# Gate tiles of a hybrid decoder layer in seven block products, and branch block sums spread over their turns

## Chip, cores and metric

The kernel runs on one core of one Trainium2 chip. The metric is the device time of one execution in microseconds; the kernel before takes 2350.80 us (median of 3 runs, 2350.69 to 2352.27). All data is fp32. Matrix products are made of three matmuls each (high x high, high x low, low x high), after an operand has been split into a rounded high part and the rest.

## What is computed

One decoder layer over 16 meta tokens and 1024 tokens, model width 1024. Cut to what matters here:

```python
h = rms_norm(x, norm1_w)
(rq, rk, rv, rg, dq, dk, dv, cb, cc, cx, gates) = [h @ w_in[:, s:e] for s, e in column_bounds()]
ret  = retention(...) ; diff = diff_attention(...) ; conv = cb * short_conv(cc * cx, conv_w)
g = sigmoid(gates).reshape(b, l, 3, 1024)
merged = g[:, :, 0] * (ret @ w_branch[0]) + g[:, :, 1] * (diff @ w_branch[1]) + g[:, :, 2] * (conv @ w_branch[2])
x = x + merged @ w_out
u = square(relu(rms_norm(x, norm2_w) @ w_up))
y = rms_norm(x + u @ w_down, final_norm_w)
```

The gates are 3 x 1024 columns of the input projection: 24 gate tiles of 128 channels by 1024 tokens.

## The kernel before

Everything is kept transposed: channels on the 128 partitions, tokens along the row. There are two ways to make a matrix product.

**Direct.** `gemm` (with `kstep`, L163 to L165) makes 128 channels by 512 tokens in 8 k-steps of 3 matmuls, so 24 matmuls; a gate tile is two of these, 48 matmuls. The weights come through `weights`: two DMAs of 256 KB each on SP's queue, a cast on ScalarE (L135), a subtraction on VectorE (L136). The right-hand side is `H`, the input times norm weight, split. The per-token factor `R` is applied to the result by `scaled` (L252).

**Seven block products.** Class `Quad` makes four tiles (4 x 128 channels by 1024 tokens) as two pairs `p`. A pair's product is a 2 x 2 block product, made with seven products of combined blocks instead of eight. The right-hand side is needed as seven combined blocks in `ORDER = ("B11", "B21", "T1", "B22", "T2", "T3", "T4")`, each split, in two 1024 KB tiles (`op`). One product of both pairs is a *turn*: 24 matmuls (L843 to L845). A quad is seven turns, 168 matmuls. `prep` combines and splits the weights two turns ahead, `copy` and `evac` take sums out of PSUM (L849 on ScalarE, L863 on VectorE), `use` does what follows.

From the gates on, the program has two parts.

The **gate stage** (24 direct tiles, in the order that the tile framework's scheduler finds) also makes the combined blocks of the three branch results for the branch products: `branch_sums(br, k)`, twelve calls, one behind each second gate tile. A call loads four 256 KB blocks, makes T1 to T4 with four VectorE operations, splits five of the seven blocks, and stores 3 MB through POOL's queue to `TD`. Gates go to `GD`. In the stage's second half the first four operands of the first branch product (`SET`) are loaded on SP's queue.

From L1243 on, the **order is written out by hand**. `steps` holds the turns; the loop at the end issues, for each turn `s`: what takes the last turn's results, the turn's matmuls, the weight preparation of turn `s + 2`, then `work[s]`, the loads of turn `s + 3`, then `fetch[s]`. Each engine runs its instructions in that order and waits at the first that isn't ready. `turn_over` loads the next right-hand side on POOL's queue while the last quad of the one before runs; T3 and T4 come whole and are split by `work` entries. The first steps are the six branch quads (branch 2, 1, 0), then the output projection, the MLP and the last product.

Rings of buffers tie the queues together: `raw` 10, `w` 5, `X` 16, `g` 3, `k` 2. A buffer that a DMA stores from is free when the store has landed.

Of the kernel before, what the change touches and what calls it, by code (L numbers as in the profile page):

```python
# [16 lines left out]
ALU = mybir.AluOpType  # L17
# [54 lines left out]
def trunk_kernel(ctx: ExitStack, tc, x, w_in, w_branch, w_out, w_up, w_down, w_down2, w_down3, vecs, lam_in, consts, y):  # L72
# [33 lines left out]
    def f32(ap):  # L106
        return ap.bitcast(F32)
# [614 lines left out]
    def ready(br, k, n, src):  # L722
        w = temp("w", [P, 2, 512], F32R)
        split(src, w[:, 0], w[:, 1])
        nc.gpsimd.dma_start(out=TD[br][n][:, :, k], in_=f32(w))

    def branch_sums(br, k):
        src = dict(BR)[br]
        b = {}
        for z in range(2):  # L730
            for j in range(2):
                b[z, j] = temp("raw", [P, 512])
                nc.sync.dma_start(out=b[z, j], in_=src[:, 4 * z + k, half(j)])
        for n, zj in PLAIN.items():
            ready(br, k, n, b[zj])
# [6 lines left out]
        for n, t in (("T3", t3), ("T4", t4)):  # L742
            nc.gpsimd.dma_start(out=TD[br][n][:, k], in_=t)
        ready(br, k, "T1", t1)
        ready(br, k, "T2", t2)

    turns[:] = TURNS
    last_sig = None
    SET = {}
    sums_todo = [(br, k) for br, _ in BR for k in range(4)]  # L750
    for n, (br, f) in enumerate((br, f) for br, _ in BR for f in range(KT)):
        wt = weights(w_in[G_GATE + br * KT + f], lo_eng=v)
        for c0, w in CH_TOK:
            pt = gemm(wt, H, c0, w)
            gt = slot("t2", [P, 512])
            scaled(gt, pt, c0, w)
            last_sig = a.activation(out=gt, in_=gt, func=AF.Sigmoid)
            nc.gpsimd.dma_start(out=GD[br][:, f, c0 - META:c0 - META + w], in_=gt)

        with tc.issue_after(getattr(last_load[0], "ins", last_load[0])):  # L760
            if n % 2 == 1:
                branch_sums(*sums_todo.pop(0))
            if 10 <= n < 18 and n % 2 == 0:

                name = ORDER[(n - 10) // 2]
                SET[name] = [opnd(True, [P, 4, 512]) for _ in range(2)]
                for z in range(2):
                    nc.sync.dma_start(out=f32(SET[name][z]), in_=TD[2][name][:, z])
# [19 lines left out]
    def at(table, s, fn):  # L788
        table.setdefault(s, []).append(fn)
# [171 lines left out]
    def last_load(name):  # L961
        open_op(SET, name, 4, False)
        if name in READY:
            for z in range(2):
                G.dma_start(out=f32(SET[name][z]), in_=TD[2][name][:, z])
        else:
            G.dma_start(out=f32(SET[name][1]), in_=TD[2][name])

    def last_split(name):
        oh, ol = SET[name]  # L970
        for k in range(4):
            split(f32(ol[:, k]), oh[:, k], ol[:, k])

    for i, name in enumerate(ORDER[4:]):
        at(fetch, i, lambda name=name: last_load(name))
        if name not in READY:
            at(work, 2 + i, lambda name=name: last_split(name))
# [143 lines left out]
    now = [0]  # L1121

    spare = [0]

    def pick_h():
        spare[0] += 1
        return "gggkk"[spare[0] % 5]
# [247 lines left out]
```

## Time and profile before

| | before |
|---|---|
| median of 3 runs | 2350.80 us |
| profiled execution | 2350.85 us |
| its span (first to last instruction) | 2348.8 us |
| TensorE busy (PE) | 2293.8 us, 98% |
| VectorE busy (DVE) | 1599.6 us, 68% |
| ScalarE busy (ACT) | 1071.3 us, 46% |
| GpSimd busy (POOL) | 496.9 us, 21% |
| DMA over the whole span | 337.57 MB, 144 GB/s |

The page's slices show PE at 9 tenths or more almost everywhere, so a time is read as a number of matmuls and what lies between them. The gate stage runs to 1346.6 us of the span, the first branch product starts at 1347.35 us. DMA is light until the gate stage and heaviest there.

### The profile page before, as it was taken

How to read it: one execution, taken by the hardware profiler on the slowest of the kernel's cores; microseconds unless marked ns; L12 is line 12 of the kernel's file. 1: busy time of each engine (PE TensorE's matmuls, PEld its weight loads, DVE VectorE, ACT ScalarE, POOL GpSimd, SP SyncE). 2: the span in 40 equal slices, each digit the busy share in tenths (PEclk: the TensorE clock that was granted, in tenths of full speed). 3: DMA queues.
4: the chain of work that ended last, by engine and by line, in shares of the span. 5: the costliest groups of instructions: out<-in, count | busy, mean ns of one | idle time of the engine just before them, and what ended most of it. 6: DMA issues, size and time to landing. Idle time of an engine off the chain costs nothing. (4 is left out here: it accounts for less than half of the span.)

```text
span 2348.8 us, 32974 instructions
## 1 busy us (share of the span) xinstructions
PE 2293.8 (98%) x11854; PEld 1992.6 (85%) x11854; DVE 1599.6 (68%) x3276; ACT 1071.3 (46%) x2079; POOL 496.9 (21%) x666
## 2 busy tenths in 40 slices
PE   7999999999999999999999999999989999999997
PEld 7999999999999899898888787778867778788876
DVE  7776777777766466667545467685776676876776
ACT  6644644654634333333333333343455565643434
POOL 2232132232221321212323210100002242200003
PEclk9999999999999999999999999999999999999999
DMA  3111111111111111114998866736425566865352
GB/s 140 33 54 38 50 54 37 55 44 44 53 42 46 54 45 46 64 55 162 336 375 329 290 247 231 309 107 206 157 66 177 186 228 246 326 232 207 108 197 72
DMA packets 126885, 337.57 MB, mean 144 GB/s; under 512 B 15744, under 2 KB 19968, under 8 KB 118144
## 3 DMA queue, kind: packets, MB, share of 16 engines
q1 hardware_dynamic: 84912, 159.27, 20.2%
q0 software_dynamic: 41808, 176.19, 19.7%
q8 instruction: 93, 1.52, 0.3%
q14 instruction: 72, 0.59, 0.1%
HBM read 224.24 MB, written 111.15 MB: 143 GB/s over the span
## 5 line engine op out<-in xcount | busy, mean ns | idle before, releaser
L163 PE MATMUL pmm<-H,whi 128*128 128x512 f32 (+3 forms) x1640 | 574.3, 352 | 12.4 <-ACT H L198 8.2
L164 PE MATMUL pmm<-H,whi 128*128 128x512 f32 (+3 forms) x1640 | 574.2, 351 | 1.4 <-DVE H L199 1.3
L165 PE MATMUL pmm<-H,wlo 128*128 128x512 f32 (+3 forms) x1640 | 573.5, 351 | 0.0
L843 PE MATMUL pb<-op,w 128*128 128x512 f32 x1176 | 465.7, 396 | 28.2 <-DVE t L863 24.2
L845 PE MATMUL pb<-op,w 128*128 128x512 f32 x1176 | 462.7, 393 | 0.0
L844 PE MATMUL pb<-op,w 128*128 128x512 f32 x1176 | 462.5, 393 | 0.0
L136 DVE TENSOR_TENSOR w<-raw,w 128x512 fp32r<-128x512 f32 (+1 forms) x400 | 263.3, 670 | 203.7 <-ACT w L135 200.9
L135 ACT CAST w<-raw 128x512 fp32r<-128x512 f32 (+1 forms) x400 | 237.4, 604 | 308.3 <-PE pb L845 111.3
L163 PEld LDWEIGHTS pmm<-H,whi 128*128 128x128 f32 x1640 | 309.5, 189 | 38.1 <-ACT H L198 8.2
L164 PEld LDWEIGHTS pmm<-H,whi 128*128 128x128 f32 x1640 | 310.4, 189 | 26.8 <-DVE H L199 2.1
L165 PEld LDWEIGHTS pmm<-H,wlo 128*128 128x128 f32 x1640 | 310.0, 189 | 24.2
L136 POOL TENSOR_TENSOR wlo<-raw,whi 128x512 fp32r<-128x512 f32 x142 | 194.0, 1367 | 593.1 <-ACT whi L135 548.1
L843 PEld LDWEIGHTS pb<-op,w 128*128 128x128 f32 x1176 | 221.8, 189 | 85.2 <-DVE t L863 20.3
L845 PEld LDWEIGHTS pb<-op,w 128*128 128x128 f32 x1176 | 221.8, 189 | 51.2 <-DVE w L136 0.9
L844 PEld LDWEIGHTS pb<-op,w 128*128 128x128 f32 x1176 | 222.0, 189 | 49.4 <-issue 0.2
L135 ACT CAST whi<-raw 128x512 fp32r<-128x512 f32 x192 | 118.7, 619 | 185.6 <-issue 69.8
L849 ACT COPY t<-pb 128x512 f32<-128x512 f32 x132 | 75.9, 584 | 109.4 <-PE pb L845 109.1
L820 DVE TENSOR_TENSOR raw<-raw,raw 128x512 f32<-128x512 f32 (+1 forms) x176 | 111.7, 664 | 10.3 <-DMA raw<-w_branch 8.6
L1133 POOL DMA_DIRECT2D d<-X x124 | 66.3, 540 | 231.4 <-DVE X L1169 119.2
L863 DVE TENSOR_TENSOR t<-pb,t 128x512 f32<-128x512 f32 x132 | 90.0, 686 | 16.3 <-PE pb L845 9.6
L380 ACT ACTIVATE B<-B,nb 128x144 f32<-128x144 f32 (+3 forms) x64 | 50.6, 791 | 99.4 <-DVE nb L379 99.2
L896 POOL DMA_DIRECT2D op<-d x46 | 24.6, 539 | 280.4 <-PE pb L845 278.5
(295 smaller groups left out, 3764.5 us busy)
## 6 DMA issues: line engine op xcount, KB each, us to landing
op<-d POOLq DMA_DIRECT2D x59, 1024.0 KB, 8.5
raw<-w_in SPq DMA_DIRECT2D x192, 256.0 KB, 2.6
d<-X POOLq DMA_DIRECT2D x140, 256.0 KB, 4.0
d<-w POOLq DMA_DIRECT2D x60, 512.0 KB, 6.7
raw<-w_up SPq DMA_DIRECT2D x76, 256.0 KB, 3.4
raw<-w_down SPq DMA_DIRECT2D x56, 256.0 KB, 5.4
d<-t POOLq DMA_DIRECT2D x50, 256.0 KB, 5.7
raw<-d SPq DMA_DIRECT2D x48, 256.0 KB, 7.5
```

Of the source, the lines that this page charges most:

```text
L135: a.copy(out=hi, in_=src)
L136: (eng or v).tensor_tensor(out=lo, in0=src, in1=f32(hi), op=ALU.subtract)
L163: nc.tensor.matmul(pt, lhsT=hi[:, s], rhs=xh[:, c0:c0 + w], start=start, stop=False)
L164: nc.tensor.matmul(pt, lhsT=hi[:, s], rhs=xl[:, c0:c0 + w], start=False, stop=False)
L165: nc.tensor.matmul(pt, lhsT=lo[:, s], rhs=xh[:, c0:c0 + w], start=False, stop=stop)
L820: comb = lambda d, x0, x1, o: v.tensor_tensor(out=d, in0=x0, in1=x1, op=o)
L843: nc.tensor.matmul(pt, lhsT=w[0][:, s], rhs=b[0][:, k], start=first, stop=False, skip_group_check=True)
L844: nc.tensor.matmul(pt, lhsT=w[0][:, s], rhs=b[1][:, k], start=False, stop=False, skip_group_check=True)
L845: nc.tensor.matmul(pt, lhsT=w[1][:, s], rhs=b[0][:, k], start=False, stop=k == nk - 1, skip_group_check=True)
L849: a.copy(out=t, in_=pt)
L863: v.tensor_tensor(out=sb, in0=pt, in1=sb, op=ALU.add)
L1133: at(fetch, now[0] + 1, lambda: G.dma_start(out=dst, in_=src))
```

## The change

Four gate tiles (the first four of branch 2) stay direct. Behind them the block sums of the *input* are made: `input_sums(k)` loads x again, multiplies by the norm weight and by `R`, makes T1 to T4, splits all seven blocks; the first four stay on the chip (`HS`), T2, T3, T4 go to DRAM (`HD`) and come back through POOL's queue. The other 20 gate tiles become five quads of the written-out order, ahead of the branch quads, with the sigmoid in `use`. The branch sums become twelve `branch_unit`s of nine operations each, dealt to the turns by the list `ROOM`; each part is stored by DMAs of 256 KB (12 a unit). The operands of the first branch product come by `turn_over` while the last gate quad runs.

```diff
-    for n, (br, f) in enumerate((br, f) for br, _ in BR for f in range(KT)):
-        wt = weights(w_in[G_GATE + br * KT + f], lo_eng=v)
+    for f in range(4):
+        wt = weights(w_in[G_GATE + 2 * KT + f], lo_eng=v)
...
         with tc.issue_after(getattr(last_load[0], "ins", last_load[0])):
-            if n % 2 == 1:
-                branch_sums(*sums_todo.pop(0))
-            if 10 <= n < 18 and n % 2 == 0:
...
+            for k in ((0, 1), (2,), (3,), ())[f]:
+                input_sums(k)
...
+    def input_sums(k):
+        b = {}
+        for z in range(2):
+            for j in range(2):
+                b[z, j] = temp("raw", [P, 512])
+                nc.sync.dma_start(out=b[z, j], in_=x[:, 4 * z + k, META + j * 512:META + j * 512 + 512])
+        for z in range(2):
+            for j in range(2):
+                f = 4 * z + k
+                v.scalar_tensor_tensor(out=b[z, j], in0=b[z, j], scalar=vec[:, V_N1 + f:V_N1 + f + 1],
+                                       in1=R[:, META + j * 512:META + j * 512 + 512], op0=ALU.mult, op1=ALU.mult)
...
+        for n, t in (("B11", b[0, 0]), ("B21", b[1, 0]), ("T1", t1), ("B22", b[1, 1])):
+            split(t, HS[n][0][:, k], HS[n][1][:, k])
...
+        for n, t in (("T2", t2), ("T3", t3), ("T4", t4)):
+            w = temp("w", [P, 2, 512], F32R)
+            split(t, w[:, 0], w[:, 1])
+            nc.gpsimd.dma_start(out=HD[n][:, :, k], in_=f32(w))
...
+    for i, name in enumerate(ORDER[4:]):
+        at(fetch, i, lambda name=name: input_load(name))
+    for br, quad in ((2, 1), (1, 0), (1, 1), (0, 0), (0, 1)):
+        q = Quad(pairs_of(w_in[G_GATE + br * KT:G_GATE + (br + 1) * KT], quad), 4, HS, gate_use(br, quad))
+        for i in range(7):
+            product_step(q, i)
...
+        def parts(n, src):
+            u = src()
+            h = temp(pick_h(), [P, 512])
+            split(u, h.bitcast(F32R), u.bitcast(F32R))
+            put(TD[br][n][:, 0, k], h)
+            put(TD[br][n][:, 1, k], u)
...
+    ROOM = (3, 1, 3, 3, 5, 2, 4)
...
+            at(fetch, turn - 2, load)
+            for fn in ops:
+                while room == 0:
+                    turn += 1
+                    room = ROOM[turn % 7]
+                at(work, turn, fn)
+                room -= 1
...
+    turn_over(len(steps) - 7, SETS[2], 4, lambda name: TD[2][name], READY, FIRST)
```

How the order moves, at the places that matter. First VectorE (DVE) behind the second direct gate tile's first half (the `scaled` of that half leads both pieces; `raw` are loaded blocks, `wlo` gate weights). Before:

```order
L252 TENSOR_TENSOR t22167_12153<-pmm2166_12128,R25_117 128x512
L136 TENSOR_TENSOR w2174_12194<-raw2170_12186,w2174_12194 128x512
L737 TENSOR_TENSOR raw2177_12206<-raw2171_12188,raw2170_12186 128x512
L136 TENSOR_TENSOR w2175_12198<-raw2172_12190,w2175_12198 128x512
L136 TENSOR_TENSOR wlo2181_12230<-raw2181_12227,whi2181_12229 128x512
L136 TENSOR_TENSOR w2176_12202<-raw2173_12192,w2176_12202 128x512
```

and of the change:

```order
L252 TENSOR_TENSOR t22194_12238<-pmm2193_12213,R25_117 128x512
L736 SCALAR_TENSOR_TENSOR raw2175_12127<-raw2175_12127,vec_79,R25_117 128x512
L736 SCALAR_TENSOR_TENSOR raw2176_12129<-raw2176_12129,vec_79,R25_117 128x512
L736 SCALAR_TENSOR_TENSOR raw2177_12131<-raw2177_12131,vec_79,R25_117 128x512
L136 TENSOR_TENSOR op2159_12047<-raw2175_12127,op2158_12046 128x512
L739 TENSOR_TENSOR raw2179_12139<-raw2176_12129,raw2175_12127 128x512
L136 TENSOR_TENSOR wlo2206_12317<-raw2206_12314,whi2206_12316 128x512
```

Where branch sums and gate work alternated, the input sums of all four k begin. Second, VectorE where the direct tiles end and the products begin (`w2465` before, `w2260` in the change, is the first weight block of the first product). Before:

```order
L740 TENSOR_TENSOR raw2420_14127<-raw2420_14127,raw2423_14133 128x512
L741 TENSOR_TENSOR raw2422_14131<-raw2422_14131,raw2420_14127 128x512
L252 TENSOR_TENSOR t22411_14024<-pmm2410_13999,R25_117 128x512
L136 TENSOR_TENSOR w2429_14158<-raw2420_14127,w2429_14158 128x512
L136 TENSOR_TENSOR w2465_14214<-raw2463_14210,w2465_14214 128x512
L136 TENSOR_TENSOR wlo2415_14066<-raw2415_14063,whi2415_14065 128x512
L252 TENSOR_TENSOR t22413_14053<-ps2412_14028,R25_117 128x512
```

and of the change:

```order
L136 TENSOR_TENSOR w2203_12300<-raw2200_12277,w2203_12300 128x512
L743 TENSOR_TENSOR raw2214_12384<-raw2214_12384,raw2212_12380 128x512
L136 TENSOR_TENSOR w2204_12304<-raw2199_12275,w2204_12304 128x512
L744 TENSOR_TENSOR raw2211_12378<-raw2211_12378,raw2214_12384 128x512
L745 TENSOR_TENSOR raw2213_12382<-raw2213_12382,raw2211_12378 128x512
L136 TENSOR_TENSOR w2216_12403<-raw2211_12378,w2216_12403 128x512
L136 TENSOR_TENSOR w2217_12407<-raw2214_12384,w2217_12407 128x512
L136 TENSOR_TENSOR w2218_12411<-raw2213_12382,w2218_12411 128x512
L136 TENSOR_TENSOR w2260_12536<-raw2258_12532,w2260_12536 128x512
```

Before, the first product's weights are split while direct tiles are still evacuated; in the change they stand behind the last input sum: 69 operations from the first L736 to `w2260`, both included, 61 of them to `w2203`. Third, POOL's queue where operands of a branch product are loaded (`op`, 1024 KB each, here T1 to T3); all other rows are stores of 256 KB. Before:

```order
L896 DMA op2563_14722<-d2146_12034 128x2048
L896 DMA op2564_14723<-d2146_12034 128x2048
L896 DMA op2572_14766<-d2147_12035 128x2048
L896 DMA op2573_14767<-d2147_12035 128x2048
L909 DMA op2594_14865<-d2149_12037 128x2048
```

and of the change (`op2613` is T3 of the first branch product, `d2154` holds blocks of the last branch):

```order
L891 DMA op2601_14389<-d2141_12029 128x2048
L962 DMA d2157_12045<-X2597_14379 128x512
L962 DMA d2152_12040<-k2598_14381 128x512
L891 DMA op2602_14390<-d2141_12029 128x2048
L904 DMA op2613_14447<-d2142_12030 128x2048
L928 DMA d2136_12024<-t2580_14303 128x512
L962 DMA d2155_12043<-g2605_14428 128x512
L962 DMA d2154_12042<-g2607_14433 128x512
```

Before, the loads follow each other alone; in the change they stand among the branch sums' stores and the gates' stores.

## Rows read from the trace of the kernel before

**Rows 1.** Page, part 1: busy time, share of the span, instructions of each engine

```profile
PE 2293.8 (98%) x11854; PEld 1992.6 (85%) x11854; DVE 1599.6 (68%) x3276; ACT 1071.3 (46%) x2079; POOL 496.9 (21%) x666
```

**Rows 2.** Timeline of PE: start us, duration us, engine, line, operation, [idle before <-releaser]

```profile
1096.77 0.39 PE L165 MATMUL pmm<-H,wlo 128*128 128x512 f32 x1
1097.46 0.39 PE L163 MATMUL ps<-H,whi 128*128 128x512 f32 x1
...
1101.62 0.39 PE L163 MATMUL ps<-H,whi 128*128 128x512 f32 x1
...
1346.17 0.40 PE L165 MATMUL pmm<-H,wlo 128*128 128x512 f32 x1
1347.35 0.50 PE L843 MATMUL pb<-op,w 128*128 128x512 f32 x1 [0.78 <-DVE t L252]
...
1350.25 0.39 PE L843 MATMUL pb<-op,w 128*128 128x512 f32 x1
...
1354.33 0.39 PE L843 MATMUL pb<-op,w 128*128 128x512 f32 x1
```

**Rows 3.** Windows: us; busy us (count) by engine; PEclk, DMA share, GB/s: gate stage, full-share stretches

```profile
1090.00:1347.00 257.00, 256.57 (x1110) 208.18 (x1109) 132.98 (x208) 91.73 (x155) 80.58 (x132) 1.00 0.92 334
1104.00:1128.00 24.00, 24.00 (x106) 19.50 (x105) 16.15 (x26) 10.22 (x18) 10.92 (x18) 1.00 1.02 391
1136.00:1160.00 24.00, 24.00 (x105) 19.50 (x105) 13.76 (x22) 9.16 (x16) 8.63 (x15) 1.00 1.00 349
1200.00:1232.00 32.00, 32.00 (x141) 25.99 (x140) 13.62 (x21) 9.79 (x17) 8.10 (x14) 1.00 1.02 399
1400.00:1432.00 32.00, 32.00 (x140) 26.07 (x139) 13.35 (x20) 7.48 (x13) 4.45 (x9) 1.00 1.02 411
```

**Rows 4.** Window of the first branch quads, columns as in Rows 3

```profile
1347.00:1546.00 199.00, 194.51 (x836) 156.27 (x837) 142.61 (x222) 70.71 (x125) 15.52 (x29) 1.00 0.66 246
```

**Rows 5.** Timeline of DVE, SP and ACT where the first branch sums begin

```profile
1097.20 0.69 DVE L252 TENSOR_TENSOR t<-pmm,R 128x512 f32<-128x512 f32 x1 [4.49 <-PE pmm L165]
1097.56 3.65 SPq L733 DMA_DIRECT2D raw<-d  x8
1100.37 0.62 ACT L135 CAST w<-raw 128x512 fp32r<-128x512 f32 x1 [7.59 <-DMA raw<-d]
1102.21 0.62 ACT L135 CAST w<-raw 128x512 fp32r<-128x512 f32 x1 [0.69 <-DMA raw<-d]
```

**Rows 6.** Timeline of DVE: operations back to back, merged (x2, x3)

```profile
1684.07 1.89 DVE L136 TENSOR_TENSOR w<-raw,w 128x512 fp32r<-128x512 f32 x3
1687.47 1.41 DVE L1073 SCALAR_TENSOR_TENSOR X<-X,vec,k 128x512 f32<-128x512 f32 x2
```

**Rows 7.** Groups by line and shape: count | busy us, mean ns | idle before

```profile
L1073 DVE SCALAR_TENSOR_TENSOR X<-X,vec,k 128x512 f32<-128x512 f32 x16 | 11.2, 747 | 0.0
```

**Rows 8.** DMA issues: out<-in, queue, count, KB each, median us from issue to landing

```profile
d<-w POOLq DMA_DIRECT2D x60, 512.0 KB, 6.7
d<-A POOLq DMA_DIRECT2D x8, 512.0 KB, 2.9
```

**Rows 9.** Page, part 5: ScalarE casts of a split, and POOL's issue of a 256 KB store

```profile
L135 ACT CAST w<-raw 128x512 fp32r<-128x512 f32 (+1 forms) x400 | 237.4, 604 | 308.3 <-PE pb L845 111.3
L1133 POOL DMA_DIRECT2D d<-X x124 | 66.3, 540 | 231.4 <-DVE X L1169 119.2
```

**Rows 10.** Timeline of PE: the longest idle time between products

```profile
1719.68 0.77 PE L843 MATMUL pb<-op,w 128*128 128x512 f32 x1 [8.04 <-DVE t L863]
```

**Rows 11.** Windows around that idle time, columns as in Rows 3

```profile
1716.00:1720.00 4.00, 0.32 (x1) 0.35 (x2) 4.00 (x7) 0.43 (x1) 0.00 (x0) 0.57 0.45 133
1720.00:1724.00 4.00, 4.00 (x12) 3.10 (x12) 0.82 (x2) 2.49 (x5) 0.00 (x0) 0.58 0.02 4
1724.00:1728.00 4.00, 4.00 (x19) 3.23 (x18) 2.44 (x5) 3.57 (x7) 0.00 (x0) 1.00 0.36 99
```

More of the change, by code (lines that the diff above doesn't have):

```diff
@@ L720, in trunk_kernel @@
     TD = {br: {n: dram([P, 2, 4, 512] if n in READY else [P, 4, 512]) for n in ORDER} for br, _ in BR}
[L722 to L728, printed above, removed]
+    FIRST = ORDER[:4]
+    HS = {n: [opnd(True, [P, 4, 512]) for _ in range(2)] for n in FIRST}
+    HD = {n: dram([P, 2, 4, 512]) for n in ORDER[4:]}
+    def input_sums(k):
         b = {}
@@ L732, in branch_sums @@
                 b[z, j] = temp("raw", [P, 512])
-                nc.sync.dma_start(out=b[z, j], in_=src[:, 4 * z + k, half(j)])
-        for n, zj in PLAIN.items():
-            ready(br, k, n, b[zj])
+                nc.sync.dma_start(out=b[z, j], in_=x[:, 4 * z + k, META + j * 512:META + j * 512 + 512])
[4 more added lines that the diff above has]
+                                       in1=R[:, META + j * 512:META + j * 512 + 512], op0=ALU.mult, op1=ALU.mult)
         t1 = temp("raw", [P, 512])
         v.tensor_tensor(out=t1, in0=b[0, 1], in1=b[0, 0], op=ALU.subtract)
+        for n, t in (("B11", b[0, 0]), ("B21", b[1, 0]), ("T1", t1), ("B22", b[1, 1])):
+            split(t, HS[n][0][:, k], HS[n][1][:, k])
         t3, t2, t4 = b[1, 1], b[0, 0], b[1, 0]
@@ L741, in branch_sums @@
         v.tensor_tensor(out=t4, in0=t4, in1=t2, op=ALU.subtract)
[L742 to L745, printed above, removed]
+        for n, t in (("T2", t2), ("T3", t3), ("T4", t4)):
+            w = temp("w", [P, 2, 512], F32R)
+            split(t, w[:, 0], w[:, 1])
+            nc.gpsimd.dma_start(out=HD[n][:, :, k], in_=f32(w))
     turns[:] = TURNS
-    last_sig = None
-    SET = {}
-    sums_todo = [(br, k) for br, _ in BR for k in range(4)]
-    for n, (br, f) in enumerate((br, f) for br, _ in BR for f in range(KT)):
-        wt = weights(w_in[G_GATE + br * KT + f], lo_eng=v)
+    for f in range(4):
+        wt = weights(w_in[G_GATE + 2 * KT + f], lo_eng=v)
         for c0, w in CH_TOK:
@@ L756, in trunk_kernel @@
             scaled(gt, pt, c0, w)
-            last_sig = a.activation(out=gt, in_=gt, func=AF.Sigmoid)
-            nc.gpsimd.dma_start(out=GD[br][:, f, c0 - META:c0 - META + w], in_=gt)
+            a.activation(out=gt, in_=gt, func=AF.Sigmoid)
+            nc.gpsimd.dma_start(out=GD[2][:, f, c0 - META:c0 - META + w], in_=gt)
         with tc.issue_after(getattr(last_load[0], "ins", last_load[0])):
-            if n % 2 == 1:
-                branch_sums(*sums_todo.pop(0))
-            if 10 <= n < 18 and n % 2 == 0:
[L765 to L768, printed above, removed]
+            for k in ((0, 1), (2,), (3,), ())[f]:
+                input_sums(k)
     gates.close()
@@ L925, in pairs_of, with gate_use, use, pick_h @@
         return [[w[2 * p + r][:, half(z)] for r in range(2) for z in range(2)] for p in (2 * quad, 2 * quad + 1)]
+    def gate_use(br, quad):
+        def use(p, r, j, src):
+            f = 4 * quad + 2 * p + r
+            g = temp("X", [P, 512]) if (r, j) == (1, 0) else src
+            a.activation(out=g, in_=src, func=AF.Sigmoid)
+            at(fetch, now[0] + 1, lambda: G.dma_start(out=GD[br][:, f, half(j)], in_=g))
+        return use
+    now = [0]
+    spare = [0]
+    def pick_h():
+        spare[0] += 1
+        return "gggkk"[spare[0] % 5]
@@ new lines, in input_load @@
+    def input_load(name):
+        open_op(HS, name, 4, False)
+        for z in range(2):
+            G.dma_start(out=f32(HS[name][z]), in_=HD[name][:, z])
+    for i, name in enumerate(ORDER[4:]):
[4 more added lines that the diff above has]
+            product_step(q, i)
+    at(work, len(steps) + 1, lambda: a.preload_act_table_set("natural_log_exp_and_others"))
@@ new lines, in branch_unit, with load, put, comb @@
+    def branch_unit(br, k):
+        b, t = {}, {}
+        def load():
+            for z in range(2):
+                for j in range(2):
+                    b[z, j] = temp("X", [P, 512])
+                    nc.sync.dma_start(out=b[z, j], in_=dict(BR)[br][:, 4 * z + k, half(j)])
+        def put(dst, src):
+            at(fetch, now[0], lambda: G.dma_start(out=dst, in_=src))
+        def parts(n, src):
[4 more added lines that the diff above has]
+            put(TD[br][n][:, 1, k], u)
+        def comb(n, x0, x1, op, out=None):
+            x0, x1 = x0(), x1()
+            t[n] = out() if out else temp("X", [P, 512])
+            v.tensor_tensor(out=t[n], in0=x0, in1=x1, op=op)
+            if n in ("T3", "T4"):
+                put(TD[br][n][:, k], t[n])
+        B = lambda z, j: lambda: b[z, j]
+        W = lambda n: lambda: t[n]
+        return load, [lambda: comb("T3", B(1, 1), B(0, 1), ALU.subtract),
+                      lambda: parts("B22", B(1, 1)),
+                      lambda: comb("T1", B(0, 1), B(0, 0), ALU.subtract, B(0, 1)),
+                      lambda: comb("T2", W("T3"), B(0, 0), ALU.add),
+                      lambda: parts("B11", B(0, 0)),
+                      lambda: parts("T1", W("T1")),
+                      lambda: comb("T4", B(1, 0), W("T2"), ALU.subtract),
+                      lambda: parts("B21", B(1, 0)),
+                      lambda: parts("T2", W("T2"))]
@@ L928, in trunk_kernel @@
+    ROOM = (3, 1, 3, 3, 5, 2, 4)
+    turn, room = 1, ROOM[1]
+    for br, _ in BR:
+        for k in range(4):
+            load, ops = branch_unit(br, k)
+            at(fetch, turn - 2, load)
[5 more added lines that the diff above has]
+                room -= 1
     M = {}
-    FIRST = ORDER[:4]
-    SETS = {2: SET, 1: {}, 0: {}}
+    SETS = {br: {} for br, _ in BR}
@@ L958, in trunk_kernel @@
             turn_over(L, SETS[nxt], 4, lambda name, nxt=nxt: TD[nxt][name], READY, FIRST)
[L961 to L977, printed above, removed]
     MO = {}
@@ L1120, in trunk_kernel @@
     FIRST_U = ["g", "g", "g", "k"]
[L1121 to L1127, printed above, removed]
     def up_use(pair):
```

2 lines of the change are left out of this document (removed).

## The prediction

> **What bounds the kernel now.** I read the page first: PE is busy for 98% of the span [rows 1], so the time is matmuls plus gaps. Then the timeline of PE in the two kinds of stage. In the gate stage 18 matmuls of 512 columns take from 1097.46 to 1101.62 us, 0.2311 us each; in a product turn 18 take from 1350.25 to 1354.33, 0.2267 us each [rows 2] (the listed 0.39 us of one overlaps its neighbours). Between the stages PE is idle 0.8 us [rows 2]. Then the windows: the gate stage is bound by PE, but its DMA share is 0.92, 334 GB/s on average [rows 3]. The transfers fit there because 24 slow direct tiles give them 257 us. The first branch quads run at a DMA share of 0.66 and PE loses 199.0 - 194.5 = 4.5 us in 199 [rows 4], 0.9 us a quad.
>
> **The matmuls.** Twenty direct tiles are 20 x 48 = 960 matmuls, 960 x 0.2311 = 221.9 us. Five quads are 5 x 168 = 840, 840 x 0.2267 = 190.4 us. All have PE to themselves, so this is on the path: -31.5 us. A turn is 24 x 0.2267 = 5.44 us.
>
> **The hand-over, on VectorE.** Up to the second direct tile's first half both kernels have the same order on PE, so its times hold: that half's last matmul starts at 1096.77 and VectorE takes the result at 1097.20 [rows 2, 5]. From there PE has 119 direct matmuls left (24 + 48 + 48, one already run): 119 x 0.2311 = 27.5 us, to 1124.6. VectorE has 69 operations before it reaches the first product's weights. It can start when a block of x has landed. These loads wait for what the first branch-sum loads waited for (the last retention stores): issued 1097.56, landed 1100.37, the next 1 to 2 us apart [rows 5]. Back to back, VectorE starts a subtraction every (1.89 - 0.69)/2 = 0.60 us, where 0.69 is one operation's length, and a scalar_tensor_tensor, 0.75 long, after 1.41 - 0.75 = 0.66 [rows 6, 7]. The 61 operations up to the split of `w2203` are 16 of the latter and 45 others: 16 x 0.66 + 45 x 0.605 = 37.8 us. With 1.3 us for the spacing of the first loads this ends at 1139.5. Then the ring of five `w` buffers decides: `w2260` needs the buffer that `w2203` is stored from, and a 512 KB store lands in 6.7 us in the loaded gate stage, in 2.9 us in a quiet one [rows 8]. I take 5, since the load here lies between. Plus 0.6 for the cast [rows 9], the first product starts at 1145.1, call it S. PE has been idle 20.5 us instead of 0.8: +19.7 us. The least is 69 x 0.605 behind 1100.4, so 1142.1, nothing waiting: +16. With the long landing (1.7 more) and, on nine of the 28 splits, the 0.77 us that a cast waits on average (308.3/400, [rows 9]) it is +28. What covers the same sums before is the direct tiles that follow; here there are none.
>
> After 8.04 us idle [rows 10] the granted clock stood at 0.57 to 0.58, so mostly at the lower level (1.2 of 2.4 GHz), and 12 matmuls started in 4 us instead of 4/0.2267 = 17.6, after which it was 1.00 again [rows 11]: 1.3 us lost for each long gap. I count two gaps (the second below): +2.6 us.
>
> **The product turns, on the engines.** A quad has 28 VectorE operations and the dealt units add 21 in seven turns: 49 x 0.605 to 0.69 = 29.6 to 33.8 us of 38.1. ScalarE has 14 splits, 6 copies, 8 sigmoids and 12 splits of parts, 40 x 0.60 = 24 us of 38.1 [rows 9]. POOL issues about 35 DMAs in them at 0.54 us, 19 of 38 us [rows 9]. All fit, VectorE with the least room. Single waits like those of the branch quads, 0.9 us a quad, would cost 5 x 0.9 = 4.5 us; they don't add to the next term, since transfers go on through them.
>
> **The transfers.** The order fixes the bytes that must move until the first branch product can be prepared. POOL's queue carries 17 operand loads of 1.049 MB and 170 stores of 0.262 MB from the first `HD` load to the store of `g2607`, whose buffer (ring `g`) ScalarE needs in turn 35; T3 of the first branch, whose split ScalarE does in turn 36, stands six stores ahead of it. SP's queue carries 98 blocks of 0.262 MB until then (48 weights, 48 branch blocks, 2 gates), of which 12 come ahead of S. Together 17 x 1.049 + (170 + 98 - 12) x 0.262 = 84.9 MB. They start about 3 us after S, when the last `HD` stores have landed. Behind the blocked cast ScalarE still has 11 operations, 6.6 us, before the copy that turn 38's first matmul waits for. Without a stall turn 38 starts at S + 38 x 5.44 = S + 206.8. So the transfers would need 84.9 MB in 206.8 - 9.6 = 197.2 us, 430 GB/s. With full share the trace shows 391, 399 and 411 GB/s, and 349 in one stretch [rows 3]. I take 400, the mean of the three, because the 349 stands alone: 84.9/0.400 = 212.3, +9.6 = S + 221.9, a stall of 15.1 us. With 411 it is 9.4 us, with 349 it is 46 us. Queued behind the waiting cast are the weight splits and PSUM copies of the next turns, and PE waits for those.
>
> The Trainium skill weighs in here ("DMA: Bandwidth & Descriptors", Specifications): it gives some 358 GB/s as a core's share of the HBM. By that the sum would be 84.9/0.358 + 9.6 - 206.8 = +40 us in this term instead of +15. The 391 to 411 GB/s of [rows 3] lie above it, so that limit is not the one that holds in this run, where one core works alone.
>
> **Sum.** -31.5 + 19.7 + 2.6 + 15.1 = +5.9 us on the profiled execution's 2350.85 us (its span of 2348.8 and 2.05 around it), which is the median of 2350.80 within 0.1. Forecast 2357 us. After turn 41 the transfers are those of before, so nothing is given back.
>
> **Rivals.**
> *The transfers keep up* (this one ends faster). For it: the needed rate is only 5% above the best stretch seen. Against: 430 GB/s over 197 us, while the best stretch of 32 us shows 411 [rows 3]. Then PE loses only its 0.9 us a quad: -31.5 + 19.7 + 1.3 + 4.5 = -6.0, 2345 us. It decides from 430 GB/s on.
> By the Trainium skill's fabric ceiling (the same page and table), 435 GB/s, this case would just come out; no stretch here reaches it.
> *The transfers run at 349 GB/s*, because the mix is mostly stores as in that stretch [rows 3]: -31.5 + 19.7 + 2.6 + 46 = +37, 2388 us. For it: three in four POOL bytes are stores of 2 KB rows. Against: 391 in the stretch before it has the same mix.
> *No long gap at the hand-over* (VectorE isn't late, because PE waits elsewhere in the direct tiles or the sums run faster), the transfers as forecast: -31.5 + 3 + 1.3 + 15.1 = -12, 2339 us. Against: 69 operations in 24 us would be 0.35 us each, and none of this size is below 0.60 [rows 6].
> *Neither stall*, matmuls and small waits alone: -31.5 + 5 = 2324 us.
> *The change doesn't remove the matmuls:* excluded, PE's row has 11605 entries before and 11485 in the change, 120 less, as 960 - 840.
>
> **How the numbers follow.** Forecast 0.55, its own range 2348 to 2368 (hand-over +16 to +28, transfers 411 to 375 GB/s). Transfers keep up 0.22, 349 GB/s 0.10, no gap 0.08, neither 0.05. The range for 8 in 10 is 2341 to 2376: it takes in the second case and part of the third. What a measurement here can tell from no change is 0.2%, 4.7 us, so 2346.1 to 2355.5 is "same". Of the forecast's 0.55, 0.41 is slower, 0.12 same, 0.02 faster; of the second case 0.14 faster, 0.07 same, 0.01 slower; the third is slower; of the fourth 0.07 faster, 0.01 same; the last is faster. That gives faster 0.26, same 0.20, slower 0.54.
>
> **What would show it.** Right: PE idle 16 to 28 us between the last direct matmul near 1124.6 and the first product, VectorE dense through it, the clock low for some 4 us behind it; DMA share 1.0 from the first product on; PE waiting some 10 us or more in turns 35 to 39, with ScalarE's cast of T3 or of a `g` buffer waiting for a DMA. Wrong: the first product before 1138, a DMA share clearly under 0.95 in the gate turns, or the first branch product reached without a gap. VectorE ending most waits inside the gate turns would mean that its 49 operations are the bound and not the bytes.

## The result, and the profile after

The changed kernel takes 2379.05 us (median of 4 runs, 2377.41 to 2382.78) against 2350.74 us: ratio 1.0124, 95% interval 1.0112 to 1.0137, slower by 28.3 us. The forecast was 2357 us, its range 2341 to 2376: the sign was right, the size was missed by 22 us. The profiled execution has a span of 2377.2 us against 2348.8, so 28.4 us are to be found.

PE's busy time fell by 20.3 us (2293.8 in [rows 1]), so its idle time grew by 48.7 us. The page's part 1:

```profile
PE 2273.5 (96%) x11734; PEld 1975.2 (83%) x11734; DVE 1672.2 (70%) x3396; ACT 1117.1 (47%) x2167; POOL 535.1 (23%) x752
```

What PE waits for from 1097 to 1420 us (engine, line, waited for: us in total, times, longest); before, up to the first branch quad, there was one wait of 0.8 us:

```profile
PE pb L838 <- ACT w L135: 23.7, 1, 23.7
PE pb L838 <- ACT t L844: 17.0, 1, 17.0
PE pb L838 <- DVE t L858: 7.1, 6, 4.2
```

The timeline of PE shows where they stand: the end of the direct tiles, the first product, two of the short waits at turn 6 of a quad, the second half of turn 34, and turn 38.

```profile
1124.17 0.39 PE L165 MATMUL ps<-H,wlo 128*128 128x512 f32 x1
1148.29 0.80 PE L838 MATMUL pb<-op,w 128*128 128x512 f32 x1 [23.73 <-ACT w L135]
...
1263.59 0.50 PE L838 MATMUL pb<-op,w 128*128 128x512 f32 x1 [0.41 <-DVE t L858]
1302.86 0.50 PE L838 MATMUL pb<-op,w 128*128 128x512 f32 x1 [0.41 <-DVE t L858]
...
1349.39 0.80 PE L838 MATMUL pb<-op,w 128*128 128x512 f32 x1 [4.21 <-DVE t L858]
1388.06 0.80 PE L838 MATMUL pb<-op,w 128*128 128x512 f32 x1 [16.97 <-ACT t L844]
```

Behind both long waits of this stretch stands ScalarE. Its timeline shows a cast into a `k` buffer that starts 6.12 us late ahead of turn 34's second half (VectorE waits for it, PE for VectorE; what released it the profile doesn't show), then a cast into a `g` buffer that waits 16.38 us for a store to land, and then the PSUM copies:

```profile
1347.39 0.62 ACT L135 CAST k<-X 128x512 fp32r<-128x512 f32 x1 [6.12 <-issue]
...
1361.57 1.30 ACT L135 CAST w<-raw 128x512 fp32r<-128x512 f32 x2 [0.98 <-DVE raw L815]
1379.25 0.62 ACT L135 CAST g<-X 128x512 fp32r<-128x512 f32 x1 [16.38 <-DMA d<-g]
1379.77 0.61 ACT L135 CAST k<-X 128x512 fp32r<-128x512 f32 x1
1380.29 1.06 ACT L844 COPY t<-pb 128x512 f32<-128x512 f32 x2
```

Windows of the stage (columns as in [rows 3]): a restart of PE, the gate turns, the moment before the operand loads begin, and from the first operand load to the cast:

```profile
1148.00:1152.00 4.00, 3.71 (x9) 2.90 (x10) 1.45 (x3) 1.48 (x3) 0.24 (x1) 0.50 1.04 398
1200.00:1300.00 100.00, 99.18 (x432) 80.52 (x431) 78.32 (x125) 55.70 (x100) 50.28 (x95) 1.00 1.01 377
1300.00:1308.00 8.00, 7.58 (x33) 5.83 (x32) 5.49 (x10) 5.73 (x11) 2.25 (x5) 1.00 0.82 279
1317.00:1379.00 62.00, 49.47 (x204) 39.50 (x202) 27.89 (x45) 19.87 (x36) 23.74 (x44) 0.91 1.02 382
```

The 28.4 us, term by term:

| term | forecast | measured | how read |
|---|---|---|---|
| matmuls | -31.5 | -27.6 | a quad is 1302.86 - 1263.59 - 0.41 = 38.86 us, 0.2313 us a matmul and not 0.2267 (0.28 us of it lie at the edges of the wait); 960 x 0.2311 - 5 x 38.86 |
| hand-over | +19.7 | +22.9 | 23.73 instead of 0.78 [rows 2] |
| stall at turns 34 to 38 | +15.1 | +21.2 | 4.21 + 16.97 |
| clock after the gaps | +2.6 | +6.6 | three restarts, 2.3, 2.4 and 1.9 us longer than the same matmuls at full clock |
| one wait a quad | 0 | +2.9 | 1.28 + 4 x 0.41 |
| behind the branch quads | 0 | +2.1 | small pieces, not assigned |
| sum | +5.9 | +28.1 | 28.4 in the spans |

The first five make 26.0; the same wait in the last branch quad stands 26.3 us later than before (1607.62 against 1581.35).

### The profile page after: what moved, and what is told of

It is laid out like the page before. It is cut to its first block, busy times and chain, and to the rows that moved or that the text cites. A ratio compares the mean times of both kernels' runs of the same rounds, so it can differ in the third digit from the quotient of the medians.

```text
span 2377.2 us, 33112 instructions
## 1 busy us (share of the span) xinstructions
PE 2273.5 (96%) x11734; PEld 1975.2 (83%) x11734; DVE 1672.2 (70%) x3396; ACT 1117.1 (47%) x2167; POOL 535.1 (23%) x752
## 3 DMA queue, kind: packets, MB, share of 16 engines
q1 hardware_dynamic: 86064, 155.07, 19.7%
## 5 line engine op out<-in xcount | busy, mean ns | idle before, releaser
L838 PE MATMUL pb<-op,w 128*128 128x512 f32 x1456 | 579.8, 398 | 76.1 <-DVE t L858 31.5
L840 PE MATMUL pb<-op,w 128*128 128x512 f32 x1456 | 575.4, 395 | 0.0
L839 PE MATMUL pb<-op,w 128*128 128x512 f32 x1456 | 575.2, 395 | 0.0
L163 PE MATMUL pmm<-H,whi 128*128 128x512 f32 (+3 forms) x1504 | 521.1, 349 | 12.4 <-ACT H L198 8.2
L164 PE MATMUL pmm<-H,whi 128*128 128x512 f32 (+3 forms) x1504 | 521.1, 347 | 1.5 <-DVE H L199 1.4
L165 PE MATMUL pmm<-H,wlo 128*128 128x512 f32 (+3 forms) x1504 | 520.3, 347 | 0.0
L838 PEld LDWEIGHTS pb<-op,w 128*128 128x128 f32 x1456 | 276.5, 190 | 148.0 <-DVE t L858 29.9
L840 PEld LDWEIGHTS pb<-op,w 128*128 128x128 f32 x1456 | 276.1, 190 | 63.6 <-DVE w L136 1.1
L839 PEld LDWEIGHTS pb<-op,w 128*128 128x128 f32 x1456 | 276.5, 190 | 61.2 <-issue 0.2
L163 PEld LDWEIGHTS pmm<-H,whi 128*128 128x128 f32 x1504 | 284.3, 189 | 32.0 <-ACT H L198 8.2
L164 PEld LDWEIGHTS pmm<-H,whi 128*128 128x128 f32 x1504 | 285.0, 190 | 20.9 <-DVE H L199 2.3
L165 PEld LDWEIGHTS pmm<-H,wlo 128*128 128x128 f32 x1504 | 284.7, 189 | 18.3
L135 ACT CAST whi<-raw 128x512 fp32r<-128x512 f32 x152 | 94.0, 619 | 138.8 <-issue 64.0
L844 ACT COPY t<-pb 128x512 f32<-128x512 f32 x162 | 93.5, 585 | 121.2 <-PE pb L840 120.5
L815 DVE TENSOR_TENSOR raw<-raw,raw 128x512 f32<-128x512 f32 (+1 forms) x216 | 137.9, 667 | 9.2 <-DMA raw<-w_branch 7.0
L858 DVE TENSOR_TENSOR t<-pb,t 128x512 f32<-128x512 f32 x162 | 109.6, 685 | 17.0 <-PE pb L840 10.5
```

The costliest lines, as they stand in the source:

```text
L163: nc.tensor.matmul(pt, lhsT=hi[:, s], rhs=xh[:, c0:c0 + w], start=start, stop=False)
L164: nc.tensor.matmul(pt, lhsT=hi[:, s], rhs=xl[:, c0:c0 + w], start=False, stop=False)
L165: nc.tensor.matmul(pt, lhsT=lo[:, s], rhs=xh[:, c0:c0 + w], start=False, stop=stop)
L815: comb = lambda d, x0, x1, o: v.tensor_tensor(out=d, in0=x0, in1=x1, op=o)
L838: nc.tensor.matmul(pt, lhsT=w[0][:, s], rhs=b[0][:, k], start=first, stop=False, skip_group_check=True)
L839: nc.tensor.matmul(pt, lhsT=w[0][:, s], rhs=b[1][:, k], start=False, stop=False, skip_group_check=True)
```

## The experiments

Two accounts of the stall are tested. Theory B, the forecast: all bytes from the first product on count, at what rate they pass. Theory L, formed after the first four runs: only those count that can't move before the first operand load, in turn 29. Beside them stands rival O: the order of POOL's queue and the ring of three `g` buffers set the stall, whatever the bytes. For the hand-over, theory H says that VectorE's row and the `w` ring set the first product.

**1. High halves only.** The kernel leaves out the stores of the low halves of the branch operands and loads the high halves twice: bytes less, the engines' work but for 60 store issues the same:

```diff
-            put(TD[br][n][:, 1, k], u)
...
-    turn_over(..., lambda name: TD[2][name], READY, FIRST)      # loads [:, 0] and [:, 1]
+    turn_over(..., lambda name: high(TD[2], name), READY, FIRST)  # loads [:, 0] twice
```

> Leaves out the 60 stores of the low halves of the branch operands that go split (15.7 MB); the loads take the high half twice, so bytes loaded and all work on the engines stay. Theory B (the stall before the first branch products is bytes through the DMA engines, 87 MB at 381 GB/s from S+3 to the cast): 71 MB need 187 us, which ends before the turns do; both gaps of PE there (4.2 and 17.0 us) fall to about 1, with two of the three clock losses of 2.4 us: 2353 us (2348 to 2359). Rival O (the order of POOL's queue and the ring of three g buffers set it, whatever the bytes): the gaps stay, 2375 to 2383.

Measured 2368.22 us, ratio to before 1.0076 (1.0061 to 1.0091): between what B (2353) and O (2375 to 2383) expected. The gate turns had room, and still PE stood 13 us at turn 38. Windows (gate turns, operand loads) and PE's timeline:

```profile
1200.00:1300.00 100.00, 99.17 (x432) 80.42 (x431) 78.04 (x125) 55.50 (x99) 32.15 (x60) 1.00 0.82 284
1332.00:1364.00 32.00, 30.89 (x133) 24.59 (x132) 15.94 (x26) 11.71 (x21) 10.93 (x20) 1.00 1.02 412
```
```profile
1378.61 0.79 PE L838 MATMUL pb<-op,w 128*128 128x512 f32 x1 [13.04 <-ACT t L844]
```

The DMA share fell from 1.01 to 0.82 where the forecast had put the shortage, and 8 of 21 us went. So the shortage is not there, and B falls in its account of place.

**2. B22 from its source.**

```diff
-    READY = ORDER[:5]
+    READY = ("B11", "B21", "T1", "T2")
...
-                      lambda: parts("B22", B(1, 1)),
+    # turn_over loads dict(BR)[br][:, 4:8, half(1)] whole; split like T3 and T4
```

> B22 of a branch is the branch's own block, so it is not stored split but loaded whole from where it already lies and split like T3 and T4: 24 stores and one operand load fewer until the first branch product, 7.3 MB. Theory B: 7.3/0.381 = 19 us off the transfers, against a stall of 21: gaps of PE there 2 to 6 us in all, one or two clock losses gone: 2358 us (2353 to 2364). Rival O: as after, 2375 to 2383. Rival V (the four more splits in turns 35 and 36 are on the path there): up to 4 x 0.6 = 2.4 us more than B.

Measured 2362.58 us, ratio 1.0048 (1.0033 to 1.0063). One gap of 6.95 us is left before turn 38 and the earlier one is gone, as both B and L say. ScalarE's timeline shows that it now waits for an operand load itself, and no longer for a `g` buffer:

```profile
1366.50 1.14 ACT L135 CAST op<-op 128x512 fp32r<-128x512 f32 x2 [8.25 <-DMA op<-d]
```

So the ring of `g` buffers isn't the whole cause: with its wait gone, the loads themselves were still late.

**3. Sums on GpSimd.**

```diff
-        v.tensor_tensor(out=t1, in0=b[0, 1], in1=b[0, 0], op=ALU.subtract)
+        nc.gpsimd.tensor_tensor(out=t1, in0=b[0, 1], in1=b[0, 0], op=ALU.subtract)
...                                              (T2, T3, T4 likewise)
```

> T1 to T4 of the input sums (16 operations) go from VectorE to GpSimd. Theory H (VectorE's row of 69 operations sets the first product): 16 x 0.605 = 9.7 us less, so PE idle 14 us instead of 23.7 at the hand-over, and the rest shifts with it: 2369 us (2366 to 2373). Rival W (the w ring and the landing of the HD stores set it): the gap stays at 22 to 25 us and the time at 2376 to 2383; GpSimd's 16 x 1.37 = 22 us in front of those stores could even add some.

Measured 2385.62 us, ratio 1.0149 (1.0134 to 1.0164), 6.6 us more than the change. Neither theory had it: H expected 2369, W at most 2383. Groups by line and shape from 1108 to 1145 us, of the change and of this run:

```profile
L736 DVE SCALAR_TENSOR_TENSOR raw<-raw,vec,R 128x512 f32<-128x512 f32 x11 | 8.2, 751 | 0.5 <-DMA raw<-xt 0.5
```
```profile
L736 DVE SCALAR_TENSOR_TENSOR raw<-raw,vec,R 128x512 f32<-128x512 f32 x12 | 15.4, 1297 | 0.0
L743 POOL TENSOR_TENSOR raw<-raw,raw 128x512 f32<-128x512 f32 x4 | 6.1, 1517 | 3.3 <-DVE op L136 3.3
```

The same operation takes 1297 instead of 751 ns on VectorE while GpSimd computes: 16 operations fewer, but the others longer, and the first product at 1155.5 us. The last casts before the first product wait for GpSimd's sums (2.51, 2.21 and 0.80 us) and then for a store (2.35 us), so the run decides neither for H nor for its rival W, the `w` ring and its stores; it shows that this cure costs more than it takes away. The Trainium skill ("Trainium Architecture — The Big Picture", What this means for kernel authors) says that the two engines share a port pair by an exclusive lock. This trace agrees that they hold each other up, 751 against 1297 ns; that it is by a lock it doesn't show.

**4. x blocks loaded earlier.**

```diff
+    mp = ctx.enter_context(tc.tile_pool(name="mp", side="left", **reuse))
     pa = ctx.enter_context(tc.tile_pool(name="pa", side="left", **reuse))
-    mp = ctx.enter_context(tc.tile_pool(name="mp", side="left", **reuse))
```

> The two pools at the start of the gate stage are opened in the other order, so the buffers of the x blocks lie where memory came free earlier; no instruction moves. The first x load then waits only for the weight loads ahead of it on its queue, about 1093 instead of 1097.2 us. Theory H: the sums start 3 to 4 us earlier and so does all that follows: 2375 us (2373 to 2378), gap 20. If something else sets the first product: unchanged, 2377 to 2383.

Measured 2378.93 us, ratio 1.0121 (1.0104 to 1.0138). The loads issued at 1093.52 instead of 1097.17, the first product came at 1146.11 instead of 1148.29; the stall grew from 21.2 to 22.9 (4.48 + 18.42). The first product follows the earlier start, as H says, but the time is a miss: 2 us gained in front were lost behind. Why the stall grew by 1.7 us stays open; L had no reason for it.

**5. Late splits.** B22, T2, T3 and T4 of the input stored whole, split in the first turns:

```diff
-        for n, t in (("T2", t2), ("T3", t3), ("T4", t4)):
-            w = temp("w", [P, 2, 512], F32R)
-            split(t, w[:, 0], w[:, 1])
-            nc.gpsimd.dma_start(out=HD[n][:, :, k], in_=f32(w))
+        for n, t in (("B22", b[1, 1]), ("T2", t2), ("T3", t3), ("T4", t4)):
+            nc.gpsimd.dma_start(out=HD[n][:, k], in_=t)
...
+        for k in range(4):
+            at(work, i + 1, lambda name=name, k=k: input_split(name, k))
```

> The input sums split only B11, B21 and T1 before the first product; B22, T2, T3 and T4 are stored whole and split in the first turns. VectorE's row to the first weights has 49 operations instead of 69, and no store of a w buffer stands in the way. Theory H (that row and the w ring set the first product): 20 x 0.605 = 12.1 us and the 2 to 4 us of the ring less: PE idle 7 to 10 us at the hand-over instead of 23.7, the first product at 1131 to 1135. Theory L (the stall before the first branch products comes from the bytes that can move only from the first operand load in turn 29 on: 22.8 MB in the 46 us that PE has): the stall keeps its 21 us and all shifts: 2362 us (2358 to 2368). Rival F (the transfers end at the same time whatever the start, being busy already): the stall grows by what the hand-over gains, over 2372.

Measured 2379.07 us, ratio 1.0123 (1.0108 to 1.0138): no gain, 17 us over what was expected. H holds for the gap, but the first quad loses it again. PE's waits in its timeline:

```profile
1132.56 0.80 PE L836 MATMUL pb<-op,w 128*128 128x512 f32 x1 [7.45 <-ACT w L135]
...
1134.22 0.80 PE L838 MATMUL pb<-op,w 128*128 128x512 f32 x1 [0.43 <-DVE w L136]
...
1148.76 0.50 PE L836 MATMUL pb<-op,w 128*128 128x512 f32 x1 [2.69 <-ACT w L135]
...
1150.77 0.80 PE L838 MATMUL pb<-op,w 128*128 128x512 f32 x1 [1.27 <-DVE w L136]
...
1162.22 0.79 PE L836 MATMUL pb<-op,w 128*128 128x512 f32 x1 [4.83 <-ACT t L842]
...
1185.08 0.79 PE L836 MATMUL pb<-op,w 128*128 128x512 f32 x1 [3.56 <-DVE t L856]
```

The first product starts 15.7 us earlier. Then come five waits, 12.8 us together, with a restart at the lower clock behind several (the matmuls listed with 0.79 or 0.80 us instead of 0.50), and the mark in the second quad (1224.33 in the change) stands at 1227.12. The splits that left the hand-over meet the units' operations in the same turns (experiment 7 moves the units). The stall stayed, 3.89 + 17.88. The time lies where rival F (over 2372) had put it, but not for F's reason: by F the stall would have grown by what the hand-over gained.

**6. Plain blocks from their source.** B11, B21 and B22 as in 2:

```diff
+    READY = ("T1", "T2")
+    FROM = {"B11": (0, 0), "B21": (4, 0), "B22": (4, 1)}
```

> B11, B21 and B22 of the branches are not stored split but loaded whole from where they lie, and split in turns 33 to 39; six of twelve stores of a unit and three of eleven loads go, and the units are through by turn 24. Theory L: from the first operand load to the last one needed 8 loads (8.4 MB), 6 stores (1.6) and 2.6 on SP's queue, 12.6 MB or 33 us at 382 GB/s, within the 46 us: gaps of PE there under 2 us each, two clock losses of 2.4 us gone: 2379 - 21 - 5 = 2353 us (2349 to 2358). Rival V (VectorE and ScalarE, 12 splits more a branch than before in the turns around a change of branch): PE waits 5 us or more there: 2358 to 2368. Rival Q (the queue order holds, not the bytes): over 2370.

Measured 2363.03 us, ratio 1.0054 (1.0039 to 1.0069). No wait at all from 1268 to 1435 us: the stall is gone. L had forecast 2353; the other 10 us were lost elsewhere: 3.02 and 0.83 us in turns 11 to 18, and 4.59 and 5.65 us at the two changes of branch, where twelve more splits meet late weights (rival V's place).

**7. Late splits and plain blocks**, the units from turn 5 on:

```diff
+    ROOM = (3, 1, 3, 3, 3, 2, 3)
+    turn, room = 5, ROOM[5 % 7]
```

> Both edits, the units dealt from turn 5 on at 18 operations in seven turns. H and L together: 2379 - 26 - 17 = 2336 us (2330 to 2345), faster than the kernel before by 0.2 to 0.9%. If the two stalls were one (a loss given back at the other place): 2350 or more.

Measured 2353.26 us, ratio 1.0012 (1.0002 to 1.0021). That is 17 us over the expected 2336, and in the place of its rival (2350 or more). Left are 6.40 + 1.27 + 1.17 + 4.93 us at the start and 4.0 + 3.1 us at the changes of branch. With the units out of the first turns, the late splits now pay: 10 us less than in 6.

**8. Late splits with B22 alone**, `ROOM = (4, 1, 3, 3, 5, 3, 4)` from turn 4:

> The late splits with B22 alone loaded whole (the second experiment), units from turn 4 on. H and L together: 2362.6 - 16 = 2347 us (2341 to 2353), so about the kernel before; part of the stall stays. If the gain at the hand-over is lost again in the stall: 2358 or more.

Measured 2363.59 us, ratio 1.0059 (1.0043 to 1.0076), 17 us over what was expected: the gain at the hand-over went into 11 us of waits in the first quad and 8.43 us at turn 38.

**9. High halves, dealt earlier.** The kernel of 1 with one line changed:

```diff
-    ROOM = (3, 1, 3, 3, 5, 2, 4)
+    ROOM = (4, 2, 4, 4, 5, 3, 5)
```

> The first experiment (low halves not stored, 15.7 MB less) with the units dealt at 27 operations in seven turns, so that they are through before the operand loads begin in turn 29: the same bytes in all, but of the stores behind the first operand load only the gates' four to six are left. Theory L (only what must move behind the first operand load counts): 11 loads, 6 stores and 2.6 MB on SP's queue are 15.7 MB, 41 us at 382 GB/s, within the 46 us that PE gives: the gap of 13.0 us of the first experiment falls under 2, with one clock loss of 2.4: 2368 - 14 = 2354 us (2349 to 2361, VectorE being fuller in the turns before). Theory B (all bytes from the first product on count, as predicted): the bytes are those of the first experiment, the gap stays 10 to 14, 2364 to 2371.

Measured 2355.96 us, ratio 1.0025 (1.0014 to 1.0036), where L expected 2354 and B at least 2364. The bytes are those of 1, and the gap of 13 us is gone: PE has no wait between 1311 and 1447 us. The windows:

```profile
1200.00:1300.00 100.00, 98.50 (x419) 77.45 (x418) 86.43 (x137) 57.11 (x105) 38.81 (x73) 1.00 0.91 320
1332.00:1364.00 32.00, 32.00 (x141) 26.04 (x140) 14.13 (x22) 13.49 (x22) 7.02 (x13) 1.00 1.02 414
```

The gate turns carry more (0.91 for 0.82), the operand loads stand alone in full share, and PE is busy through them. This is the run that decides against B: not how many bytes, but how many behind the first operand load. What holds the operand loads back changed as well. In the change four of POOL's operand loads stand 1.9 to 2.3 us until earlier ones have landed and one stands 0.5 us for PE; here none waits for a landing, and five wait 1.5 to 4.5 us for PE to release the buffer. One of each, first the change, then this run:

```profile
1330.03 0.55 POOL L891 DMA_DIRECT2D op<-d  x1 [2.22 <-DMA op<-d]
```
```profile
1346.99 0.54 POOL L904 DMA_DIRECT2D op<-d  x1 [4.53 <-PE pb L840]
```

The run moves stores and blocking casts together, so it doesn't tell L from the part of O that concerns the ring of `g` buffers. Experiment 2 says that the ring isn't all of it; a longer ring alone wasn't tried.

**10. Eight direct tiles**, four quads, late splits, plain blocks; branch 2's sums in the direct stage:

```diff
-    for f in range(4):
+    for f in range(8):
...
+            for k in ((), (), (), (0,), (1,), (2,), (3,), ())[f]:
+                branch_sums(2, k)
...
-    for br, quad in ((2, 1), (1, 0), (1, 1), (0, 0), (0, 1)):
+    for br, quad in ((1, 0), (1, 1), (0, 0), (0, 1)):
```

> Branch 2's eight gate tiles direct, 16 tiles in four quads; late splits, plain blocks; branch 2's sums in the direct stage, the other eight units from turn 4 on at 16 operations in seven turns. Against the change: one quad less is 4 x 48 - 168 = 24 matmuls more, +5.5 us; the sums' rows on VectorE (93 operations x 0.61 = 57 us from 1100) now end before the direct tiles do (1169), so the 23.7 us gap and its clock loss of 2.4 go but for 1 us, -25; no stall before the first branch product, -26 with its clock losses; the waits at the branch changes of the seventh experiment, +9: 2379 + 5.5 - 25 - 26 + 9 = 2342 us (2337 to 2349), faster than the kernel before. If hand-over or operand loads still stall, 2352 or more.

Measured 2350.45 us, ratio 1.0000 (0.9991 to 1.0008): the same as before, 8 us over the forecast. The hand-over is 1.95 us, turn 38's place has no wait; the changes of branch still cost 4.10 and 3.33 us.

**11. The same, with two shifts:**

```diff
-            for k in ((), (), (), (0,), (1,), (2,), (3,), ())[f]:
+            for k in ((), (), (), (0,), (1,), (2,), (), ())[f]:
...
-                at(fetch, L + i + 1, lambda name=name: whole_load(name))
+                at(fetch, L + i + 1 + (left_names is FIRST and name == "T4"), lambda name=name: whole_load(name))
```

> The tenth experiment with two shifts: only three of branch 2's sums stay in the direct stage (the fourth becomes the first unit, so the weight loads of the last direct tiles and of the first product come earlier on SP's queue), and T4 of a branch is loaded one turn later, so that the 256 KB weight loads at a change of branch share the DMA engines with one 1 MB load less. If the waits left in the tenth (2.3 + 1.1 + 2.0 us in the direct stage, 4.1 and 3.3 at the branch changes) are the queueing of small loads behind large ones: 5 to 8 us less, 2344 us (2340 to 2347), faster than the kernel before by about 0.3%. If they come from VectorE and ScalarE: unchanged, 2348 to 2352.

Measured 2347.14 us, ratio 0.9983 (0.9974 to 0.9992): faster than before, but the waits at the changes of branch stayed (4.61 and 3.02 us), so one large load less in front of the small ones did not help there. SP's timeline shows another candidate: a pair of gate loads that holds the queue 15.8 us, with the next branch's weights behind it.

```profile
1383.83 0.86 SPq L817 DMA_DIRECT2D raw<-w_branch  x2
1384.84 15.75 SPq L1045 DMA_DIRECT2D g<-d  x2
1400.64 0.90 SPq L817 DMA_DIRECT2D raw<-w_branch  x2
```

**12. Gate loads in two rings:**

```diff
-                    gt[p, r, j] = temp("g", [P, 512])
+                    gt[p, r, j] = temp(pick_h(), [P, 512])
```

> The eleventh experiment with the gate loads of the branch products spread over the g and k rings (five buffers instead of three). In the eleventh SP's queue stands 15.8 us at a gate load that waits for its g buffer, with the w_branch loads of the next branch behind it; those land late, ScalarE's casts wait for them and PE loses 4.6 and 3.0 us at the two changes of branch, with a clock loss each. If that wait is the cause: both gaps under 2, 2347 - 5 to 9 = 2340 us (2337 to 2343), 0.4% faster than the kernel before. If the cause is the 1 MB loads on the DMA engines in front of the small ones: gaps unchanged, 2345 to 2349.

Measured 2336.74 us, ratio 0.9942 (0.9929 to 0.9956), 14 us faster than the kernel before and 42 less than the change, and 0.3 us under the expected 2337 to 2343. PE's timeline at the two changes of branch:

```profile
1415.26 0.50 PE L857 MATMUL pb<-op,w 128*128 128x512 f32 x1 [0.61 <-ACT op L135]
...
1494.06 0.49 PE L857 MATMUL pb<-op,w 128*128 128x512 f32 x1 [0.18 <-ACT op L135]
```

4.61 and 3.02 us became 0.92 and 0.50 (each with a short second wait, 0.31 and 0.32). The wait for the `g` buffer was the cause; with it about 10 us went, the restarts at the lower clock among them.

## Why the prediction was right and wrong

**The hand-over** came as forecast, in place and in cause. PE ended its direct tiles at 1124.6 and the first product started at 1148.29, not 1145.1; the bound of +28 held. VectorE worked without a break of over 0.5 us from 1102.8 to 1143.8. Then the cast of the last input part and that of the first product's weights each waited for a store of a `w` buffer to land:

```profile
1145.41 0.62 ACT L135 CAST w<-raw 128x512 fp32r<-128x512 f32 x1 [2.44 <-DMA d<-w]
1147.62 0.62 ACT L135 CAST w<-raw 128x512 fp32r<-128x512 f32 x1 [1.59 <-DMA d<-w]
```

Experiments 5 and 10 show two ways of removing most of it: fewer operations in the row, or more direct tiles over it.

**The stall** was forecast at the right instruction: turn 38's first matmul, behind PSUM copies, behind a ScalarE cast that waits for a `g` store. But the step that made its size failed: that the 84.9 MB which must move from 3 us after S on, in 197.2 us, set the stall. Experiment 1 took 15.7 MB out of that account, at 381 GB/s (the mean from 1151 to 1379) worth 41 us, more than the whole stall, and the stall of 21 us lost 8. The window of 1300 to 1308, share 0.82, says the same of the change itself: just ahead of the operand loads the transfers were not behind. What can't be spread is what stands behind the first operand load. That load can't go before PE has finished with its buffer, in turn 28, and the blocked cast is due in turn 35, T3's split in turn 36. From the load's issue at 1316.89 to the store of `g2607` POOL's queue carries 11 loads of 1.049 MB and 29 stores of 0.262, SP's some 14 blocks: 22.8 MB. At the 382 GB/s of that window it takes 60 us, where 46 are left (1316.89 to 1362.87, when ScalarE reaches the cast; turn 34's wait lies in these 46). That makes 14 of the cast's 16.38 us. The 15 us of the forecast were near turn 38's 17 by chance: a stretch too long with a rate too high. Experiment 9, with the bytes of experiment 1 in another order, settles that the sum over all bytes was the wrong one. How much of the stall the ring of `g` buffers adds to the bytes behind the first load stays open.

**The rate**, 382 GB/s over the 62 us, lies below the 391 to 411 that were averaged; the 349 of [rows 3] was no outlier: windows of 8 us at full share pass 343 GB/s (1372 to 1380) to 422 (1324 to 1332) in the change. It is above the 358 GB/s of the Trainium skill ("DMA: Bandwidth & Descriptors", Specifications), as the forecast had said of the rows before.

**The matmuls** were 3.9 us too cheap. Their number was right (the page counts 11854 and 11734, 120 less), but the 18 matmuls read from the first product turn are of the faster part of a quad, four turns of seven. In the change, the timeline of PE in turns 0 to 3 of a quad, and in turns 4 to 6:

```profile
1276.11 0.39 PE L838 MATMUL pb<-op,w 128*128 128x512 f32 x1
...
1280.19 0.39 PE L838 MATMUL pb<-op,w 128*128 128x512 f32 x1
...
1295.74 0.39 PE L840 MATMUL pb<-op,w 128*128 128x512 f32 x1
...
1299.94 0.39 PE L840 MATMUL pb<-op,w 128*128 128x512 f32 x1
```

18 take 4.08 us and 18 take 4.20: 0.2267 and 0.2333. Four turns of the one and three of the other make 38.56 us, 0.2295 a matmul, and the wait of a quad costs 0.28 us more at its edges than the 0.41 listed; with that the quad comes to 0.2313. The direct tiles' matmuls take 0.2311. So a product matmul saves next to nothing over a direct one, and the gain is in their number, 120 x 0.231 = 27.7 us. [rows 4] gave a warning: 194.51 us of busy time for the 836 matmuls listed are 0.2327 each.

**The clock** was counted for two gaps at 1.3 us; there were three, at about 2.2. The 12 matmuls in 4 us of [rows 11] were read from a window's edge; matmul by matmul the first restart takes 5.04 us for 12 that take 2.72 at full clock (granted clock 0.50 in the window of 1148 to 1152, the lower level, 1.2 GHz).

**The wait once a quad** was dropped because transfers go on through it. That was wrong where transfers are not the bound: from turn 6 to turn 34 they were in time, and the 2.9 us were on the path.

All five errors have one sign. The sign of the forecast held since the two large losses were found from the order, but it was partly luck: without the stall's 15.1 us, which rest on the step that failed, the sum is -9.2. The forecast's own range was also added up too narrow at the top: with the +28 of the hand-over and the 29 of 375 GB/s the terms give 2379, not 2368. And its chances add up to 0.28 for faster and 0.52 for slower, not 0.26 and 0.54.

## What to carry to other kernels

Bytes are counted against the stretch in which they may move: find the earliest issue of the last group of loads (here the release of the operand buffers) and what its queue carries from there to the instruction that waits, not the mean over a stage. Work that is moved from a covered place to a hand-over between two kinds of work needs a cover of its own; the direct tiles were that cover. Of the versions tried the best has eight of them and four quads, with late splits, plain blocks and gate loads in two rings; the number of direct tiles was not varied by itself. A duration that is multiplied by 840 is read from a whole period, not from its first 18.

## What was not expected of the hardware

The spacing of matmuls of one shape has two values in the same granted clock of 1.00, 0.2267 and 0.2333 us. It changes at turn 4 of each gate quad of the change, and of the branch quads before it too (in the stretches looked at, 1148 to 1430 us, and 1347 to 1590 us before). Turns 0 to 3 read operand buffers of one pool (`pa`), turns 4 to 6 of the other (`pb`); whether the place of the buffer is the cause was not tried. And a VectorE operation on 128x512 fp32 grew from 751 to 1297 ns on average beside GpSimd arithmetic (experiment 3).
